# A hybrid streaming encoder step: how the first rows are loaded and summed, a second plain unit in layer 0's output projection, and the last sums and stores

## The chip, the cores and the metric

The kernel runs on one core of a Trainium2 chip. The metric is the device time of one execution, in microseconds, smaller being better. Where the text says PE, DVE, ACT, POOL and SP, it means the five engines as the profile names them: PE multiplies matrices, DVE does elementwise work, ACT applies functions of one input, POOL is a second and slower elementwise engine, and SP issues transfers. Every engine works through its own list of instructions strictly in order.

## The reference

The model is one recurrent layer and one attention layer on 544 tokens (512 of a prompt and 32 of a running stream), 2048 features wide, in float32:

```python
def rms_norm(x, g):                       # over the 2048 features of a token
    return x * lax.rsqrt(jnp.mean(x * x, axis=-1, keepdims=True) + EPS) * g

# layer 0
proj = rms_norm(x, norm_rec) @ w_in_rec            # 2048 -> 2048 + 2048 + 1024 + 1024
xa, ga, xb, gb = split(proj)
ya = rg_lru(causal_conv(xa))                       # gated linear recurrence over time
yb = pool_mix(xb)                                  # trailing means, a map per group
x  = x + concat([ya * silu(ga), yb * silu(gb)]) @ w_out_rec      # 3072 -> 2048
# layer 1
q, k, v, gt = split(rms_norm(x, norm_att) @ w_in_att)            # 2048 -> 4 * 2048
x  = x + (stick_breaking_attention(q, k, v) * silu(gt)) @ w_out_att
y  = rms_norm(x, norm_final)
```

The outputs are `y`, the keys and values, and the last states of the recurrence, the convolution and the pooling.

## The kernel before

Features lie on the 128 partitions and the 544 tokens along the free axis, so that a matrix of 2048 features is 16 "rows" of 128 x 544. A token half has 272 columns. Every float32 operand of a big matmul is split into a rounded high part and a low part (`wsplit`, `split`, `xsplit`: ACT makes the high part, DVE subtracts to get the low one), and one product is three matmuls (`mm3`, L107 to L110: high by high, high by low, low by high).

The projections go by **units** of two blocks of 128 output features by two token halves. A `plain_unit` does, for each of the first 12 input rows, two blocks, two halves and three matmuls, in chunks of 6 rows; a `unit` replaces the 8 block products of these 12 rows by 7, Strassen's way, with sums and differences of weight blocks (DVE, L385 to L400) and of input quarters. Those sums of inputs are made once for each input matrix by `sums_by_pairs`: its loads fetch quarter blocks from DRAM in three rounds, its makes form three sums a round (L283 to L285) and split them (L230, L231), and `three` makes a fourth (L299). The tiles are named T1 to T4 (`xh`, `xl` on the page). Input rows past the 12th are the `xp` rows, done by `rest` plainly. Weight chunks come into a pool of 7 raw buffers (`wraw`), and their split parts into 3 pairs (`wh`, `wl`). Accumulators are 4 PSUM banks (`pp`).

The program is written in a tile framework which inserts the waits and orders each engine's list by a schedule of its own; `tc.high_priority()` draws an instruction forward in it. **Hooks**, a dictionary from a place in a unit to functions, put other work at the chunks of a unit (L329 `run`).

Four stretches matter here.

- **Start.** Unit 0 (`plain_unit(srcs[0], keep, ...)`, L648) needs the 16 rows of x, scaled by `norm_rec`. `load_x` (L489) takes a buffer of an 8-buffer pool (`T`), loads a row, and makes its scaled high and low parts. `squares` (ACT, L483) puts each row's squares into a tile of a 5-buffer pool (`ev`), and `add_squares` sums over the features on PE: `rstd_add` (L137) multiplies by a two-column matrix of ones, 5 token blocks for each of the 16 rows. `rstd_sums` then computes 1/rms (L148 to L153) and diagonal matrices of it (L158), and `rstd_spread` (L168, L170) multiplies these by ones, which puts 1/rms of every token on all partitions; it is copied into `rbc`. Unit 0's results are kept unscaled until then.
- **Layer 0's output projection.** `u == 0` is a plain unit whose hooks bring in the 12 `xp` rows (16 of the 21 `T` buffers hold eight of them for good) and also run the loads and makes of the sums. `u == 1` to 7 are Strassen units.
- **Start of attention.** Head 0 begins with a plain unit; its hooks load and split the `xp` rows, run the sums of x2g (`one`, `two`, `three`), and at places 3 and 4 `rstd_sums` and the copy of the spread 1/rms to `rbc`, which every result of the unit is multiplied by (L449).
- **End.** The last output projection leaves 4 rows, done for 16 blocks in the first token half and then in the second (L1148). Each block's sum is squared on ACT and added to `sqacc` by POOL (L1165), but the last, whose squares stay by themselves; `finish` multiplies by 1/rms and stores on SP's queue (L1142). In the second half, the first half's 16 finishes run beside the matmuls, and the second half's 16 come after them.

## Time and profile before

| what | value |
|---|---|
| median of three runs | 2011.17 us (2004.25, 2011.17, 2015.48) |
| profiled execution, its own time | 2008.65 us |
| its span, first to last instruction | 2006.9 us |
| PE busy | 1941.0 us, 97% |
| DVE busy | 1446.4 us, 72% |
| ACT busy | 919.3 us, 46% |
| POOL busy | 261.6 us, 13% |
| mean granted PE clock | 0.98 |

The span and the execution's own time differ by 1.75 us. A busy PE does not mean that it works at its best pace, since overlapping matmuls and a lowered clock both count as busy; the number of instructions in a stretch, the (x...) of the view by stretches, tells more. PEclk there is the granted share of the full PE clock. In a row of the timeline, the bracket at the end gives the idle time before the instruction and what ended it.

### The profile page before, as it was taken

How to read it: one execution, taken by the hardware profiler on the slowest of the kernel's cores; microseconds unless marked ns; L12 is line 12 of the kernel's file. 1: busy time of each engine (PE TensorE's matmuls, PEld its weight loads, DVE VectorE, ACT ScalarE, POOL GpSimd, SP SyncE). 2: the span in 40 equal slices, each digit the busy share in tenths (PEclk: the TensorE clock that was granted, in tenths of full speed). 3: DMA queues.
4: the chain of work that ended last, by engine and by line, in shares of the span. 5: the costliest groups of instructions: out<-in, count | busy, mean ns of one | idle time of the engine just before them, and what ended most of it. 6: DMA issues, size and time to landing. Idle time of an engine off the chain costs nothing.

```text
span 2006.9 us, 37651 instructions
## 1 busy us (share of the span) xinstructions
PE 1941.0 (97%) x15082; PEld 1919.6 (96%) x15082; DVE 1446.4 (72%) x2318; ACT 919.3 (46%) x1284; POOL 261.6 (13%) x369
## 2 busy tenths in 40 slices
PE   8999999999999889999799999999999999999996
PEld 8999999998999789999799999999999999999996
DVE  4465668669888665556788888888888888874347
ACT  5466666665434443334444453444444444442233
POOL 0021113112010000101111110110111101110013
PEclk8899999999999989999899999999999999999998
DMA  5254434333335654446433343333333333365334
GB/s 181 63 157 144 141 117 137 101 88 103 106 105 179 206 151 141 144 142 212 137 101 102 118 126 103 101 112 116 98 105 107 121 106 101 101 213 183 106 99 148
DMA packets 129951, 257.04 MB, mean 128 GB/s; under 512 B 15920, under 2 KB 40752, under 8 KB 129776
## 3 DMA queue, kind: packets, MB, share of 16 engines
q1 hardware_dynamic: 129696, 254.37, 42.0%
q8 instruction: 118, 1.93, 0.4%
q14 instruction: 57, 0.47, 0.1%
q0 software_dynamic: 80, 0.28, 0.0%
HBM read 217.64 MB, written 36.95 MB: 127 GB/s over the span
## 4 chain that ended last, share of the span: by engine, by line
PE 76%; DVE 12%; issue 5%; DMA 5%; ACT 1%; POOL 0%; SPq 0%; DVEq 0%; ACTq 0%; POOLq 0%
PE pp L108 23%; PE pp L110 23%; PE pp L109 23%; DVE wl L204 3%; DMA wraw<-in_w_in_att 2%; PE pg L137 1%; DMA wraw<-in_w_in_rec 1%; DVE xl L231 1%; DMA T<-x2g 1%; PE pm L109 1%; DVE big L898 1%; PE pm L110 1%; PE pm L108 1%; PE pa L915 1%; DVE e L447 1%
## 5 line engine op out<-in xcount | busy, mean ns | idle before, releaser
L108 PE MATMUL pp<-xh,wh 128*128 128x272 f32 x3180 | 925.4, 292 | 21.0 <-ACT xh L230 10.7
L110 PE MATMUL pp<-xh,wl 128*128 128x272 f32 x3180 | 921.3, 290 | 4.2 <-DVE wl L204 3.9
L109 PE MATMUL pp<-xl,wh 128*128 128x272 f32 x3180 | 921.0, 290 | 1.3 <-DVE xl L231 1.3
L203 ACT ACTIVATE wh<-wraw 128x768 fp32r<-128x768 f32 (+2 forms) x622 | 485.1, 782 | 839.5 <-PE pp L109 603.8
L204 DVE TENSOR_TENSOR wl<-wraw,wh 128x768 fp32r<-128x768 f32 (+2 forms) x622 | 546.2, 881 | 240.1 <-ACT wh L203 237.4
L108 PEld LDWEIGHTS pp<-xh,wh 128*128 128x128 f32 x3180 | 605.2, 191 | 23.7 <-ACT xh L230 11.6
L110 PEld LDWEIGHTS pp<-xh,wl 128*128 128x128 f32 x3180 | 604.2, 190 | 7.0 <-DVE wl L204 6.8
L109 PEld LDWEIGHTS pp<-xl,wh 128*128 128x128 f32 x3180 | 605.0, 190 | 3.2 <-DVE xl L231 2.1
L110 PE MATMUL pp<-xp,wl 128*128 128x272 f32 x1152 | 334.3, 290 | 2.5 <-DVE wl L204 2.2
L108 PE MATMUL pp<-xp,wh 128*128 128x272 f32 x1152 | 332.3, 290 | 3.0 <-ACT xp L230 3.0
L109 PE MATMUL pp<-xp,wh 128*128 128x272 f32 x1152 | 332.1, 289 | 0.0
L108 PEld LDWEIGHTS pp<-xp,wh 128*128 128x128 f32 x1152 | 218.9, 191 | 4.4 <-ACT xp L230 3.3
L110 PEld LDWEIGHTS pp<-xp,wl 128*128 128x128 f32 x1152 | 218.8, 190 | 3.6 <-DVE wl L204 3.6
L109 PEld LDWEIGHTS pp<-xp,wh 128*128 128x128 f32 x1152 | 218.3, 190 | 0.2 <-DVE xp L231 0.2
L447 DVE TENSOR_TENSOR e<-pp,e 128x272 f32<-128x272 f32 x156 | 65.6, 438 | 42.5 <-PE pp L110 37.9
L408 DVE TENSOR_TENSOR e<-pp,e 128x272 f32<-128x272 f32 x184 | 75.4, 430 | 5.6 <-PE pp L110 4.6
L109 PE MATMUL pp<-T,wh 128*128 128x272 f32 x256 | 73.0, 288 | 0.0
L110 PE MATMUL pp<-T,wl 128*128 128x272 f32 x256 | 72.9, 287 | 0.0
L108 PE MATMUL pp<-T,wh 128*128 128x272 f32 x256 | 71.9, 288 | 0.0
L230 ACT ACTIVATE xh<-T 128x544 fp32r<-128x544 f32 x72 | 46.5, 654 | 52.7 <-DVE T L283 18.2
L209 ACT ACTIVATE T<-T 128x544 fp32r<-128x544 f32 (+1 forms) x72 | 45.1, 646 | 44.1 <-DMA T<-in_cv 16.1
L231 DVE TENSOR_TENSOR xl<-T,xh 128x544 fp32r<-128x544 f32 x72 | 51.7, 735 | 12.7 <-ACT xh L230 12.5
(242 smaller groups left out, 2141.3 us busy)
## 6 DMA issues: line engine op xcount, KB each, us to landing
wraw<-in_w_in_att SPq DMA_DIRECT2D x128, 384.0 KB, 3.5
wraw<-in_w_in_rec SPq DMA_DIRECT2D x96, 384.0 KB, 3.4
wraw<-in_w_out_rec SPq DMA_DIRECT2D x64, 384.0 KB, 3.4
wraw<-in_w_in_att SPq DMA_DIRECT2D x64, 256.0 KB, 3.3
wraw<-in_w_in_rec SPq DMA_DIRECT2D x48, 256.0 KB, 3.3
wraw<-in_w_out_att SPq DMA_DIRECT2D x32, 384.0 KB, 4.0
T<-in_xT SPq DMA_DIRECT2D x44, 272.0 KB, 4.6
T<-mixd SPq DMA_DIRECT2D x36, 272.0 KB, 4.5
```

The lines of the kernel that those rows point to most:

```text
L108: nc.tensor.matmul(out, wh, xh, start=start, stop=False)
L109: nc.tensor.matmul(out, wh, xl, start=False, stop=False)
L110: nc.tensor.matmul(out, wl, xh, start=False, stop=stop)
L137: nc.tensor.matmul(ps[:, 1, 256 + 2 * c:258 + 2 * c], a[:, st:st + P], ones[:, :2], start=first and c == 0, stop=last and c == n - 1)
L203: nc.scalar.activation(hi, src, AF.Copy)
L204: nc.vector.tensor_tensor(lo, src, f(hi), ALU.subtract)
L209: nc.scalar.activation(a, src, AF.Copy)
L230: nc.scalar.activation(h, src, AF.Copy)
L231: nc.vector.tensor_tensor(l, src, f(h), ALU.subtract)
L408: nc.vector.tensor_tensor(sm[name], acc[p], sm[other], ALU.add)
L447: nc.vector.tensor_tensor(src, bk, addend, ALU.add)
L898: nc.vector.tensor_tensor_scan(inc[:, o:o + w][:, ::-1], s, s, 1.0, ALU.mult, ALU.min)
```

## The change

Four edits, each in one of the four stretches.

1. **Start.** All 16 rows of x are loaded without an arithmetic instruction between them, into six tiles that lie where the sums T1 to T3 will be later (`room`), and not into the `T` pool; the six weight chunks of unit 0 are issued between them. Scaling (`scale_rows`) comes afterwards and at the hooks. The sum of squares is formed by adding tiles: ACT squares a row, DVE adds it to `sqacc` (`sq_add(..., eng=nc.vector)`), and PE multiplies by ones once, 5 blocks in all, inside `rstd_sums`. `rest` can now take an early chunk.
2. **Output projection of layer 0.** `u == 1` is a plain unit too, and carries the loads and makes of the sums that were in `u == 0`; `three` moves to `u == 2`.
3. **Start of attention.** `rstd_sums` moves from hook 3 of head 0 to hook 1, and `rbc` is copied by ACT with priority instead of by DVE.
4. **End.** The additions to `sqacc` go from POOL to DVE; the squares of the last two blocks (before: of the last one) stay by themselves and are summed by PE; in the second half, odd blocks are stored from ACT's queue and even ones from SP's.

```diff
@@ -334,7 +334,7 @@
-    def rest(src, m, accs, starts, hooks):
+    def rest(src, m, accs, starts, hooks, early=()):
 
         n = len(XP)
         step = n // -(-n // NS)
@@ -342,7 +342,7 @@
             if c:
                 run(hooks, (m, c))
             with tc.high_priority():
-                hi, lo = wsplit(raw(src[:, 2 * NS + c:2 * NS + c + step]))
+                hi, lo = wsplit(early.pop(0) if early else raw(src[:, 2 * NS + c:2 * NS + c + step]))
             for j in range(step):
                 xh, xl = XP[c + j]
                 for acc, hs, st in zip(accs, (H1, H2), starts):
@@ -364,7 +364,7 @@
         for m in range(2):
             run(hooks, 4 + m)
             if more:
-                rest(srcs[m], m, accs[2 * m:2 * m + 2], (False, False), hooks)
+                rest(srcs[m], m, accs[2 * m:2 * m + 2], (False, False), hooks, early)
             for hf in range(2):
                 out(2 * m + hf, accs[2 * m + hf], None)
 
@@ -471,47 +471,51 @@
         xgd = dp.tile([P, 2 * NS, N], F32, tag="xgd", name="xgd")
         for s in (B11, B12, B21, B22):
             fresh(s)
+        rps = two_banks()
         xraw = []
-
-        rps = two_banks()
-        blocks = token_blocks(0, N)
-        sqs = {}
+        room = [xs.tile([P, 3, N], F32, tag=f"{q}{s}", name=nm("xraw")) for s in (T1, T2, T3) for q in ("xh", "xl")]
+
+        def load_rows(k0, k1):
+            for k in range(k0, k1):
+                xraw.append(room[k // 3][:, k % 3, :])
+                nc.sync.dma_start(xraw[k], xT[:, k, :])
+
+        def scale_rows(k0, k1):
+            for k in range(k0, k1):
+                xk, gk = xraw[k], vcol("norm_rec", k)
+                if k < 2 * NS:
+                    j = k % NS
+                    parts = [(XH[s][:, j, :], XL[s][:, j, :], h)
+                             for s, h in zip((B11, B12) if k < NS else (B21, B22), (H1, H2))]
+                else:
+                    hi, lo = fresh_row(k - 2 * NS)
+                    parts = [(hi, lo, slice(0, N))]
+                for hi, lo, h in parts:
+                    nc.scalar.activation(hi, xk[:, h], AF.Identity, scale=gk)
+                    nc.vector.scalar_tensor_tensor(lo, xk[:, h], gk, f(hi), ALU.mult, ALU.subtract)
 
         def squares(k0, k1):
             for k in range(k0, k1):
-                sqs[k] = ev()
-                nc.scalar.activation(sqs[k][:, :N], xraw[k], AF.Square)
-
-        def add_squares(k0, k1):
-            for k in range(k0, k1):
-                rstd_add(rps, blocks, sqs[k], k == 0, k == KT - 1)
-
-        def load_x(k):
-            xk = T()
-            nc.sync.dma_start(xk, xT[:, k, :])
...
-            xraw.append(xk)
-
-        def load_rows(k0, k1):
-            for k in range(k0, k1):
-                load_x(k)
-
-        early = [raw(w_in_rec[0, :, :NS])]
-        load_rows(0, 6)
-        early.append(raw(w_in_rec[1, :, :NS]))
-        squares(0, 5)
-        load_rows(6, 8)
-        early.append(raw(w_in_rec[0, :, NS:2 * NS]))
+                sq_add(k, xraw[k], eng=nc.vector)
+
+        def chunk(m, c):
+            early.append(raw(w_in_rec[m, :, c * NS:min((c + 1) * NS, KT)]))
+
+        early = []
+        load_rows(0, 1)
+        chunk(0, 0)
+        load_rows(1, 6)
+        chunk(1, 0)
+        load_rows(6, 9)
+        chunk(0, 1)
+        load_rows(9, 12)
+        chunk(1, 1)
+        load_rows(12, KT)
+        chunk(0, 2)
+        chunk(1, 2)
+        scale_rows(0, 6)
 
         def scaled_row(k):
 
@@ -646,12 +650,12 @@
 
         srcs = [(w_in_rec[2 * u], w_in_rec[2 * u + 1]) for u in range(24)]
         plain_unit(srcs[0], keep, {
-            1: lambda: (add_squares(0, 5), early.append(raw(w_in_rec[1, :, NS:2 * NS])), load_rows(8, 11), squares(5, 9)),
-            2: lambda: (add_squares(5, 9), load_rows(11, 14), squares(9, 13)),
-            3: lambda: (add_squares(9, 13), load_rows(14, 16), squares(13, 16)),
-            4: lambda: add_squares(13, 16)}, early=early)
+            1: lambda: scale_rows(6, 9), 2: lambda: (scale_rows(9, 12), squares(0, 3)),
+            3: lambda: (scale_rows(12, KT), squares(3, 6)), 4: lambda: squares(6, 9),
+            5: lambda: squares(9, 12)}, early=early)
+        squares(12, KT)
         box = []
-        hk = {0: decay_rates, 1: lambda: box.append(rstd_sums(rps, 0, N, [])),
+        hk = {0: decay_rates, 1: lambda: box.append(rstd_sums(rps, 0, N)),
               2: lambda: (nc.vector.tensor_copy(rbc, rstd_spread(rps, box[0])), late0()),
               4: lambda: back(0, c0)}
         one, two, three = sums(xgd)
@@ -823,14 +827,18 @@
                     1: lambda: (made_rows(), mixed_rows(4, 7)),
                     2: lambda: (made_rows(), mixed_rows(7, 10)),
                     3: lambda: (made_rows(), mixed_rows(10, 12)),
-                    4: lambda: (made_rows(), load(), loads[0]()),
-                    (0, 6): lambda: (makes[0](), loads[1]()),
-                    5: lambda: (makes[1](), loads[2]()),
-                    (1, 6): lambda: (makes[2](), lastload())})
+                    4: lambda: (made_rows(), load())})
+            elif u == 1:
+                plain_unit(srcs, out, {
+                    0: loads[0],
+                    1: lambda: (makes[0](), loads[1]()),
+                    2: lambda: (makes[1](), loads[2]()),
+                    3: lambda: makes[2](),
+                    4: load, 5: lastload})
             else:
                 hk = {2: load}
-                if u == 1:
-                    hk[1] = three
+                if u == 2:
+                    hk[0] = three
                 last = u == KT // 2 - 1
                 if last:
                     quarters(x2g, hk)
@@ -1045,9 +1053,14 @@
             if h == 0:
                 rps = att_tile()
                 box = []
-                with_hooks(ha, {0: [lambda: pend.append(rows(x2g))], 1: [one, lambda: pend.pop()()], 2: [two],
-                                3: [lambda: box.append(rstd_sums(rps, 0, N)), three],
-                                4: [lambda: nc.vector.tensor_copy(rbc, rstd_spread(rps, box[0]))]})
+
+                def spread_rbc():
+                    with tc.high_priority():
+                        nc.scalar.activation(rbc, rstd_spread(rps, box[0]), AF.Copy)
+                with_hooks(ha, {0: [lambda: pend.append(rows(x2g))],
+                                1: [lambda: box.append(rstd_sums(rps, 0, N)), one, lambda: pend.pop()()],
+                                2: [two], 3: [three],
+                                4: [spread_rbc]})
             else:
                 with_hooks(ha, {1: [lambda: (v_turn(prev), w_turn(prev))], 4: [lambda: av(h - 1, prev)]})
             if hh == 0 and G > 0:
@@ -1139,17 +1152,18 @@
             plain_unit(srcs, out, with_hooks({}, hk), more=False)
         pend.pop()()
 
-        def finish(m, hf, r):
+        def finish(m, hf, r, queue=nc.sync):
             s = (H1, H2)[hf]
             o = x3[m][:, s]
             nc.vector.scalar_tensor_tensor(o, o, vcol("norm_final", m), r, ALU.mult, ALU.mult)
-            nc.sync.dma_start(y[:, m, s], o)
+            queue.dma_start(y[:, m, s], o)
 
         for hf, s in enumerate((H1, H2)):
+            accs = [sqacc]
             for m in range(KT):
                 ps = bank()
                 if hf == 1 and m == 2:
-                    rst = rstd_sums(rps, 0, HN, accs)
+                    rst = rstd_sums(rps, 0, HN, done)
                 if hf == 1 and m == 6:
                     nc.scalar.activation(rbc[:, H1], rstd_spread(rps, rst), AF.Copy)
                 with tc.high_priority():
@@ -1159,22 +1173,22 @@
                 nc.vector.tensor_tensor(x3[m][:, s], x3[m][:, s], ps, ALU.add)
                 if m == 0:
                     nc.scalar.activation(sqacc[:, s], x3[m][:, s], AF.Square)
-                elif m < KT - 1:
+                elif m < KT - 2:
                     sq = e()
                     nc.scalar.activation(sq, x3[m][:, s], AF.Square)
-                    nc.gpsimd.tensor_tensor(sqacc[:, s], sqacc[:, s], sq, ALU.add)
+                    nc.vector.tensor_tensor(sqacc[:, s], sqacc[:, s], sq, ALU.add)
                 else:
-                    last = T()
-                    nc.scalar.activation(last[:, s], x3[m][:, s], AF.Square)
-                    accs = [sqacc, last]
+                    accs.append(T())
+                    nc.scalar.activation(accs[-1][:, s], x3[m][:, s], AF.Square)
                 if hf == 1 and m >= 8:
                     finish(2 * (m - 8), 0, rbc[:, H1])
                     finish(2 * (m - 8) + 1, 0, rbc[:, H1])
+            done = accs
             rps = att_tile()
         rst = rstd_sums(rps, HN, N, accs)
         r = rstd_spread(rps, rst)
         for m in range(KT):
-            finish(m, 1, r)
+            finish(m, 1, r, (nc.sync, nc.scalar)[m % 2])
 
 
 # ---- launch ---------------------------------------------------------------
```

**Where the instructions stand.** Outside the four stretches the lists of all engines agree. Three places show the difference.

PE at the start of the program, before: after the first 36 matmuls (unit 0, first chunk), the products of the squares with ones (`pg<-ones,ev`, five each) stand between the matmuls (`pp`).

```order
L110 MATMUL pp_196<-xh_3_111,wl_200 128x272
L137 MATMUL pg_117<-ones,ev_158 128x2 x5
L108 MATMUL pp_197<-xh_1_109,wh_292 128x272
L137 MATMUL pg_117<-ones,ev_160 128x2 x5
L109 MATMUL pp_197<-xl_2_110,wh_292 128x272
L110 MATMUL pp_197<-xh_1_109,wl_293 128x272
L108 MATMUL pp_198<-xh_3_111,wh_292 128x272
```

And now: one such group is left, after 228 matmuls (the 192 of unit 0 and 36 of unit 1), and the spread of 1/rms follows 36 matmuls later.

```order
L110 MATMUL pp_500<-xh_3_111,wl_543 128x272
L137 MATMUL pg_117<-ones,sqacc 128x2 x5
L108 MATMUL pp_501<-xh_1_109,wh_601 128x272
...
L110 MATMUL pp_502<-xh_3_111,wl_602 128x272
L168 MATMUL pg_117<-big_593,ones 128x128 x4
L170 MATMUL pg_117<-big_593,ones 128x32
```

So 75 small products are gone from PE, and 264 big matmuls stand ahead of the spread, as before. What PE waits for at L137 is now the last addition to `sqacc`; DVE's list holds the additions between the splits of the next unit's weights (`wl`):

```order
L123 TENSOR_TENSOR sqacc<-sqacc,ev_448 128x544
L204 TENSOR_TENSOR wl_602<-wraw_599,wh_601 128x768
L123 TENSOR_TENSOR sqacc<-sqacc,ev_451 128x544
L559 TENSOR_SCALAR lt_509<-lt_509 128x16
L123 TENSOR_TENSOR sqacc<-sqacc,ev_454 128x544
```

DVE in layer 0's output projection, before: the second and third round of sums (`T`) stand in one piece, with no weight split between them, in front of unit 1's next weight split.

```order
L231 TENSOR_TENSOR xl_1152_8001<-T_8015,xh_1151_8000 128x544
L283 TENSOR_TENSOR T_8079<-T_8079,T_8075 128x544
L284 TENSOR_TENSOR T_8075<-T_8075,T_8077 128x544
L231 TENSOR_TENSOR xl_1154_8003<-T_8079,xh_1153_8002 128x544
L285 TENSOR_TENSOR T_8077<-T_8079,T_8077 128x544
L231 TENSOR_TENSOR xl_1150_7999<-T_8075,xh_1149_7998 128x544
...
L204 TENSOR_TENSOR wl_8323<-wraw_8320,wh_8322 128x768
```

And now, inside the plain unit 1, each round has splits of that unit's weights around and between its sums:

```order
L204 TENSOR_TENSOR wl_8335<-wraw_8332,wh_8334 128x768
L283 TENSOR_TENSOR T_8134<-T_8134,T_8130 128x544
L284 TENSOR_TENSOR T_8130<-T_8130,T_8132 128x544
L231 TENSOR_TENSOR xl_1162_8120<-T_8134,xh_1161_8119 128x544
L285 TENSOR_TENSOR T_8132<-T_8134,T_8132 128x544
L231 TENSOR_TENSOR xl_1158_8116<-T_8130,xh_1157_8115 128x544
L204 TENSOR_TENSOR wl_8390<-wraw_8387,wh_8389 128x768
```

The sums are now ahead of unit 2, which is the first to use them, and not in the middle of unit 1.

DVE at the start of attention, before: the steps to 1/rms (`rs`) and its diagonals (`big<-ident,rs`) are spread among the sums of x2g.

```order
L148 TENSOR_SCALAR rs_71<-pa_10953 128x5
L204 TENSOR_TENSOR wl_11280<-wraw_11277,wh_11279 128x512
L283 TENSOR_TENSOR T_11012<-T_11012,T_11008 128x544
L284 TENSOR_TENSOR T_11008<-T_11008,T_11010 128x544
L150 RECIPROCAL rs_73<-rs_72 128x5
...
L151 TENSOR_TENSOR rs_74<-rs_73 128x5
L299 TENSOR_TENSOR T_11117<-T_11117,xh_1575_11086 128x544
...
L158 TENSOR_SCALAR big_11176<-ident,rs_73 128x128 x5
```

And now: they stand together, ahead of the `xp` rows and of all sums.

```order
L148 TENSOR_SCALAR rs_71<-pa_10866 128x5
L204 TENSOR_TENSOR wl_11112<-wraw_11109,wh_11111 128x768
L150 RECIPROCAL rs_73<-rs_72 128x5
L151 TENSOR_TENSOR rs_74<-rs_73 128x5
L152 SCALAR_TENSOR_TENSOR rs_74<-rs_74,rs_71 128x5
L153 SCALAR_TENSOR_TENSOR rs_73<-rs_74,rs_73 128x5
L158 TENSOR_SCALAR big_10932<-ident,rs_73 128x128 x5
L231 TENSOR_TENSOR xp_10957<-T_10871,xp_10956 128x544
```

On PE the spread moved with them, from behind the plain unit's last matmul to its second chunk.

11 lines of the change are left out of this document (removed).

## The prediction

> **What bounds the kernel now.** I began with the span in 40 slices, to see where PE is not at its best, then took the view by stretches for those slices, and in each stretch the timeline and the groups, to find what PE waited for.
>
> ```profile
> PE   8999999999999889999799999999999999999996
> PEclk8899999999999989999899999999999999999998
> ```
>
> PE is full in nearly all slices, so it is the bound; what can be won lies in slices 0, 1, 13, 14, 19 and 39. The change's four stretches are just these. The view by stretches (time, busy time and instruction count of each engine, granted PE clock, DMA share, GB/s) prices them:
>
> ```profile
> core 0: us, PE busy (x) PEld busy (x) DVE busy (x) ACT busy (x) POOL busy (x), PEclk, DMA share, GB/s
> 0.00:40.00 40.00, 32.75 (x187) 32.38 (x187) 19.51 (x60) 21.38 (x42) 1.33 (x25) 0.79 0.63 218
> 40.00:80.00 40.00, 40.00 (x281) 40.00 (x281) 12.47 (x27) 14.39 (x24) 1.04 (x3) 0.83 0.17 51
> 680.00:720.00 40.00, 28.08 (x166) 26.23 (x166) 25.92 (x39) 16.36 (x26) 1.87 (x1) 0.83 0.59 176
> 960.00:1000.00 40.00, 26.17 (x185) 25.74 (x184) 33.27 (x59) 18.33 (x28) 2.10 (x3) 0.79 0.42 134
> 1000.00:1040.00 40.00, 40.00 (x322) 39.87 (x321) 32.63 (x51) 16.86 (x22) 4.34 (x6) 1.00 0.32 92
> 1960.00:2006.90 46.90, 30.58 (x233) 29.38 (x231) 36.45 (x80) 17.12 (x36) 13.74 (x15) 0.84 0.45 147
> ```
>
> Undisturbed, PE does 322 matmuls in 40 us: 0.1244 us each. At 40 to 80 it is "busy" throughout but does 281, at clock 0.83: busy there does not mean fast. All times below are of the profiled execution (2008.65 us); it lies 2.5 us under the median of the three runs, which spread over 11 us, and I add nothing for that.
>
> **Start.** The groups up to 75 us, the spread of 1/rms (L168), three stretches of 5 us, and one row of PE's and one of SP's timeline (start, duration, line, operands, count, idle before):
>
> ```profile
> L137 PE MATMUL pg<-ones,ev 128*128 128x2 f32 x160 | 23.2, 270 | 0.0
> L502 DVE SCALAR_TENSOR_TENSOR xl<-T,vec,xh 128x272 fp32r<-128x272 f32 x24 | 10.3, 495 | 4.8 <-ACT xh L501 4.8
> L502 DVE SCALAR_TENSOR_TENSOR xp<-T,vec,xp 128x544 fp32r<-128x544 f32 x4 | 3.0, 780 | 0.4 <-ACT xp L501 0.2
> L204 DVE TENSOR_TENSOR wl<-wraw,wh 128x768 fp32r<-128x768 f32 (+1 forms) x10 | 9.0, 902 | 23.7 <-ACT wh L203 23.7
> L168 PE MATMUL pg<-big,ones x8: 271/275/275, 75.0 to 75.8; 128*128 128x128 f32 x8
> 10.00:15.00 5.00, 5.00 (x33) 5.00 (x33) 4.76 (x16) 5.00 (x11) 0.00 (x0) 1.00 1.04 392
> 25.00:30.00 5.00, 5.00 (x25) 5.00 (x25) 0.33 (x1) 0.99 (x2) 0.00 (x0) 0.53 0.00 0
> 40.00:45.00 5.00, 5.00 (x42) 5.00 (x42) 1.31 (x3) 1.10 (x3) 0.19 (x1) 1.00 0.02 4
> 7.25 1.01 PE L108 MATMUL pp<-xh,wh 128*128 128x272 f32 x2 [7.25 <-ACT xh L501]
> 30.77 3.90 SPq L491 DMA_DIRECT2D T<-in_xT  x8
> ```
>
> The last eight rows of x are not even asked for until 30.77, because a weight load ahead of them in SP's list waits for a buffer; from 25 to 30 nothing moves at all. Meanwhile PE makes two-column products, a whole 128x128 weight load for each, and its clock stands at 0.53. Before the spread at 75.0 stand 264 big matmuls, which at the full pace take 264 x 0.1244 = 32.8 us; with 7.3 us of idleness ahead, the other 75 - 7.3 - 32.8 = 35 us are the small products (23.2 by their row) and half clock: clocks of 0.79 and 0.83 over 40 us each mean (0.21 + 0.17) x 40 x 2 = 30 us at half, in which 15 us are lost (some of these inside the small products' row).
>
> Now: the same 264 matmuls, 7.3 us of idleness (the first row's load and scaling are still what it takes to begin), 2.4 us for some 23 matmuls at half clock until it rises, as I read it from 33 matmuls instead of 40 in 10 to 15, and one group of five doubled small products, 10 of 160 records, 1.2 us. PE alone would reach that group, behind 228 matmuls, at 7.3 + 2.4 + 28.4 = 38.1. But the group needs the last addition on DVE, and these 15 additions are new there:
>
> ```profile
> L284 DVE TENSOR_TENSOR T<-T,T 128x544 f32<-128x544 f32 x3 | 2.2, 719 | 0.0
> ```
>
> A 128x544 sum of two tiles takes 0.72: 10.8 us. In front of the last one DVE also has the low parts (10.3 + 3.0), some nine weight splits (8.1) and small work (about 2): 34 us, from 7.3 on, so 41 if DVE never starves. PE waits about 3 us, does 36 matmuls (4.5 us) while DVE forms the diagonals, and spreads at about 47: **28 us** earlier. With no wait for DVE and some overlap it is 31. The bad end is 18: DVE starves for 5 us (it waited 4.8 and 0.4 for ACT before) and PE's clock falls in that wait. The loads are no limit, as the 16 rows (4.5 MB) and six chunks (2.1 MB) at 392 GB/s take 17 us and now stand in one run, ahead of the rows' use. ACT's 16 squares only move.
>
> [...]
>
> **Output projection.** Unit 1's PE rows, and the two DVE sums that PE waited for, then the unit's end:
>
> ```profile
> 691.65 0.39 PE L108 MATMUL pp<-xh,wh 128*128 128x272 f32 x1 [1.03 <-DVE T L806]
> 698.81 0.82 PE L108 MATMUL pp<-xh,wh 128*128 128x272 f32 x2 [4.63 <-ACT xh L230]
> 704.41 0.39 PE L108 MATMUL pp<-xh,wh 128*128 128x272 f32 x1 [1.58 <-ACT xh L230]
> 713.42 0.59 PE L108 MATMUL pp<-xh,wh 128*128 128x272 f32 x1 [4.14 <-ACT xh L230]
> 702.95 0.72 DVE L283 TENSOR_TENSOR T<-T,T 128x544 f32<-128x544 f32 x1 [3.43 <-DMA T<-mixd]
> 711.96 0.72 DVE L283 TENSOR_TENSOR T<-T,T 128x544 f32<-128x544 f32 x1 [4.05 <-DMA T<-mixd]
> 744.35 0.81 DVE L806 TENSOR_TENSOR T<-T,pp 128x272 f32<-128x272 f32 x2 [2.36 <-PE pp L110]
> ```
>
> Unit 1 stops for each round of sums, whose loads of quarter blocks come late, about 9 us apart. Its 270 matmuls are worth 33.6 us but took 744.3 - 691.7 = 52.6, with spells of half clock after each stop. The change gives up one of eight products (18 more matmuls, 2.2 us) and needs no sum: 288 x 0.1244 = 35.8, a gain of 16.8. The sums remain on DVE, in unit 1, and weight splits of the same unit are queued behind the ones that wait for a load (0.87 to 0.95 us each, 3 pairs of buffers as slack). Three rounds 9 us apart fit into 36 us; I charge 2.3 us for splits made late by a waiting sum: **14.5 us**. Good end 16.8 plus the 1.0 at its head, 18; bad end 8, if two of the three stops (4.6 and 4.1 us) come back through the weight splits.
>
> **Attention.**
>
> ```profile
> 972.04 0.29 PE L110 MATMUL pp<-xp,wl 128*128 128x272 f32 x1
> 984.12 2.05 PE L168 MATMUL pa<-big,ones 128*128 128x128 f32 x8 [11.80 <-issue]
> 988.47 0.56 PE L108 MATMUL pp<-xh,wh 128*128 128x272 f32 x1 [2.04 <-DVE T L449]
> 1000.90 0.29 PE L109 MATMUL pp<-xl,wh 128*128 128x272 f32 x1
> 967.87 0.18 DVE L150 RECIPROCAL rs<-rs 128x5 f32<-128x5 f32 x1
> 978.44 0.16 DVE L151 TENSOR_TENSOR rs<-rs 128x5 f32<-128x5 f32 x1
> 983.75 1.06 DVE L158 TENSOR_SCALAR big<-ident,rs 128x128 f32<-128x128 f32 x5
> ```
>
> PE ends the plain unit at 972.3 and has nothing until 1/rms is spread at 984.1; all four banks wait to be multiplied by it. The chain on DVE starts in time, but its short steps (0.15 to 0.18) stand in line behind sums: 10.6 us between two of them. Together, and ahead of the sums, the chain should be over before the unit is. PE's stop of 11.8 + 2.0 goes, and with it the slow restart (0.79 over this stretch). It does not all become gain: DVE, 33.3 of 40 us busy here, has the same sums to make before PE can go on into the Strassen part, and the chain was not what delayed these. Counting its list as it now stands from about 966.5 on (18 sums and splits at no more than the 0.72 of the row above, 4 weight splits at 0.90, 5 results of 272 columns at about 0.42), the sums of the second quarter are ready at about 985. The products that use these end at 1000.90 before, some 100 matmuls behind the stop; they would end at about 990. From these 11 us I take 3 off for the backlog that DVE carries into the next part: **8 us**. Ends: 4 (DVE is the bound through the whole stretch, only the second stop and the slow clock go), 13 (the whole stop goes). The copy to `rbc`, 0.71 on DVE, costs ACT, 18 of 40 us busy, nothing.
>
> **Tail.**
>
> ```profile
> 1974.99 0.49 DVE L1145 SCALAR_TENSOR_TENSOR T<-T,vec,rbc 128x272 f32<-128x272 f32 x1
> 1976.59 1.01 DVE L1145 SCALAR_TENSOR_TENSOR T<-T,vec,rbc 128x272 f32<-128x272 f32 x1
> 1990.36 0.83 PE L137 MATMUL pa<-ones,sqacc 128*128 128x2 f32 x6 [2.51 <-POOL sqacc L1165]
> 1995.41 4.17 DVE L1145 SCALAR_TENSOR_TENSOR T<-T,vec,pa 128x272 f32<-128x272 f32 x10 [1.17 <-PE pa L170]
> 1995.93 4.75 SPq L1146 DMA_DIRECT2D out_y<-T  x10
> 2000.78 3.12 SPq L1146 DMA_DIRECT2D out_y<-big  x6
> ```
>
> PE's last sum waits 2.5 us for POOL; that goes. DVE takes over 28 additions of 272 columns, about 0.42 each (10 finishes of that size take 4.17): 14 in this half, 5.9 us, on an engine busy 36.45 of 46.9; against that, finishes that coincide with POOL take twice as long (1.01 against 0.49), and this goes. SP issues 16 stores in 7.9 us; DVE's 16 finishes at 0.42 take 6.7, so two queues save at most 1.2. Sum of +2.5, +1.2 and about +2 of collisions, less DVE's part that isn't hidden (about 4): **1.5 us**; between 4 (all additions hidden) and -1.
>
> [...]
>
> **Sum.** 28 + 14.5 + 8 + 1.5 = 52; 2008.65 - 52 = **1957 us**. All good ends: 66, 1943. All bad ends: 18 + 8 + 4 - 1 = 29, 1980.
>
> **Rivals.**
>
> - *Half clock stays in the start.* If the slow spells belong to something other than the small products and the stops (the first microseconds of any program, say), 15 us are still lost, the spread comes at 62 instead of 47, and the sum is 37: 1972. For it: the clock is below 1 in 30 of the first 80 us. Against: in 40 to 45 it is 1.00 again, so it is no matter of age. Chance 0.12.
> - *DVE becomes the bound in three places.* The additions make 34 us of DVE work in a row at the start (gain 20), sums block splits in unit 1 (8), backlog in attention (4), nothing in the tail: 32, so 1977. For it: DVE is 83% busy in 960 to 1000. Against: in 40 to 80 it is 31% busy. Chance 0.18.
> - *Slower: PE's clock falls.* With its pauses gone, PE works without rest; if the granted clock over the rest (1941 us busy) fell by 52/1941 = 2.7%, from 0.98 to 0.955, all is lost, and beyond 3.3% it is slower than 2020. Against it: 1000 to 1040 has PE full and clock 1.00. Chance 0.02.
> - *The change doesn't do what it says.* Rows of x could still wait on SP. In the new list of SP they stand behind one another with only fresh buffers between, so this is in the 0.12 of the first rival's time.
>
> **How the numbers follow.** Forecast 0.63, its own range 1948 to 1968; all terms at their good ends 0.05 (1943); the rivals 0.12, 0.18 and 0.02. The range 1944 to 1977 leaves out the slow case, half of the fast one, and the upper part of the DVE case. A difference under 0.5% (10 us) can't be told from no change here, so faster means under 2001 and slower over 2021. Every case but the third rival is well under 2001: faster 0.96, same 0.025, slower 0.015.
>
> **What would show it.** Start: L168 at 44 to 50 us instead of 75, L137 with 10 rows in place of 160, and a clock near 1.00 in 15 to 80; a wait of PE at L137 for DVE's `sqacc` over 5 us shows the second rival. Output projection: no stop over 2 us within unit 1, some 320 matmuls in 680 to 720 (shifted). Attention: no idle time ahead of L168; PE's idle before the Strassen part under 4 us. Tail: L1145 at 0.4 to 0.5 throughout, L137 released by ACT or DVE in under 1 us. What would make it wrong: a spread later than 57, PE idle in unit 1 behind DVE's `wl` (L204), or a mean clock below 0.98.

## The result, and the profile after

The changed kernel takes 1954.53 us (median of four runs, 1951.20 to 1959.63), the kernel before 2009.39 in the runs beside it (four runs, 2004.25 to 2015.48): a ratio of 0.9728, 95% interval 0.9692 to 0.9764, 54.9 us less where 52 were forecast. The profiled executions differ by 2008.65 - 1951.20 = 57.4 us, and so do the spans (2006.9 and 1949.5).

The profile's page of the changed kernel, busy tenths of PE and granted clock in 40 slices:

```profile
PE   8999999999999999999999999999999999999997
PEclk9999999999999999999999999999999999999998
```

The dips in slices 1, 13, 14 and 19 are gone; what is left is the first slice and the last. The view by stretches of the changed kernel (busy time and count of each engine, PE clock, DMA share, GB/s):

```profile
core 0: us, PE busy (x) PEld busy (x) DVE busy (x) ACT busy (x) POOL busy (x), PEclk, DMA share, GB/s
0.00:40.00 40.00, 32.94 (x242) 32.67 (x243) 33.39 (x78) 32.05 (x61) 1.51 (x26) 1.00 0.72 248
40.00:80.00 40.00, 40.00 (x323) 40.00 (x321) 28.02 (x55) 26.70 (x36) 8.17 (x10) 1.00 0.37 99
660.00:700.00 40.00, 38.57 (x308) 38.57 (x309) 30.57 (x44) 17.15 (x26) 2.73 (x2) 1.00 0.64 199
920.00:960.00 40.00, 37.22 (x286) 35.85 (x285) 37.39 (x61) 22.14 (x32) 11.37 (x6) 1.00 0.44 133
```

And the kernel before, over the 40 us that stand for 660 to 700 there:

```profile
690.00:730.00 40.00, 27.23 (x159) 25.36 (x159) 30.20 (x48) 16.49 (x25) 1.87 (x1) 0.83 0.56 167
```

PE does 308 matmuls in place of 159 in the output projection's unit 1, and 323 in place of 281 at 40 to 80, at a clock of 1.00 in both. DVE is now busy 33.4 of the first 40 us (19.5 before): it took the additions over.

Where the time came from is read by looking up the same PE instruction in both timelines and taking the difference of its start:

| the same instruction of PE | before, us | after, us | difference |
|---|---|---|---|
| first big matmul | 7.25 | 7.06 | 0.2 |
| a gate product of the recurrence, behind unit 1 and others | 333.68 | 302.73 | 31.0 |
| first of the output projection's unit 1 | 691.65 | 661.43 | 30.2 |
| first of its unit 2 | 744.51 | 697.56 | 47.0 |
| shortly before attention | 950.03 | 904.25 | 45.8 |
| in head 0, behind its Strassen part | 1076.85 | 1021.34 | 55.5 |
| 60 us before the end | 1939.91 | 1883.72 | 56.2 |
| end of the last big matmul | 1987.84 | 1931.00 | 56.8 |
| span | 2006.9 | 1949.5 | 57.4 |

So the start gives 31, the output projection 15.6 (unit 2 gives 1.2 of the 16.7 back), attention some 10, the end about 1.

The start in the changed kernel: the groups of small products and of additions, the spread of 1/rms, the last addition on DVE and PE's one group of small products:

```profile
L137 PE MATMUL pg<-ones,sqacc 128*128 128x2 f32 x10 | 1.2, 243 | 0.0
L123 DVE TENSOR_TENSOR sqacc<-sqacc,ev 128x544 f32<-128x544 f32 x15 | 10.9, 724 | 0.1
L168 PE MATMUL pg<-big,ones x8: 271/275/275, 44.0 to 44.8; 128*128 128x128 f32 x8
37.51 0.73 DVE L123 TENSOR_TENSOR sqacc<-sqacc,ev 128x544 f32<-128x544 f32 x1
38.41 1.17 PE L137 MATMUL pg<-ones,sqacc 128*128 128x2 f32 x10
```

The last addition ends at 38.24 and PE arrives at 38.41: no wait at all, but no slack on DVE either. At the start of attention, the chain on DVE, the copy on ACT, and three of the four waits of about 1 us that PE has left there (the fourth, 0.95, is ahead of the sum over the features, for POOL):

```profile
909.47 0.18 DVE L150 RECIPROCAL rs<-rs 128x5 f32<-128x5 f32 x1
909.69 0.20 DVE L151 TENSOR_TENSOR rs<-rs 128x5 f32<-128x5 f32 x1
914.54 0.61 ACT L1059 ACTIVATE rbc<-pa 128x544 f32<-128x544 f32 x1
929.82 0.36 PE L108 MATMUL pp<-xh,wh 128*128 128x272 f32 x1 [0.94 <-DVE T L449]
937.25 0.39 PE L108 MATMUL pp<-xh,wh 128*128 128x272 f32 x1 [1.43 <-ACT xh L230]
969.81 0.39 PE L110 MATMUL pp<-xh,wl 128*128 128x272 f32 x1 [0.96 <-DVE wl L204]
```

The two steps that stood 10.6 us apart are 0.22 apart, 1/rms is spread while the plain unit runs, and the stops of 11.8 and 2.0 us have become 0.9 and 1.4.

### The profile page after: what moved, and what is told of

It is laid out like the page before. It is cut to its first block, busy times and chain, and to the rows that moved or that the text cites. A ratio compares the mean times of both kernels' runs of the same rounds, so it can differ in the third digit from the quotient of the medians.

```text
span 1949.5 us, 37355 instructions
## 1 busy us (share of the span) xinstructions
PE 1907.7 (98%) x14962; PEld 1886.7 (97%) x14962; DVE 1449.8 (74%) x2343; ACT 915.5 (47%) x1281; POOL 242.7 (12%) x341
## 4 chain that ended last, share of the span: by engine, by line
PE 49%; DVE 9%; DMA 4%; issue 3%; ACT 1%; POOL 0%; SPq 0%; DVEq 0%; ACTq 0%; POOLq 0%
PE pp L108 15%; PE pp L110 15%; PE pp L109 15%; DVE wl L204 3%; DMA wraw<-in_w_in_att 2%; DVE big L906 1%; PE pm L109 1%; DMA T<-x2g 1%; DVE xl L231 1%; PE pm L110 1%; PE pm L108 1%; PE pa L923 1%; DMA T<-mixd 1%; ACT wh L203 0%; PE pa L109 0%
## 5 line engine op out<-in xcount | busy, mean ns | idle before, releaser
L209 ACT ACTIVATE T<-T 128x544 fp32r<-128x544 f32 (+1 forms) x72 | 45.2, 645 | 46.1 <-DMA T<-in_cv 17.5
L1091 POOL COPY kn<-T 128x32 f32<-128x32 f32 x16 | 20.6, 1286 | 326.9 <-DVE T L449 326.9
```

The lines of the kernel that those rows point to most:

```text
L209: nc.scalar.activation(a, src, AF.Copy)
L1091: nc.gpsimd.tensor_copy(kn[:, hh, :], k_[:, SEQ:])
```

## The experiments

Each kernel is a change to the changed kernel, and a difference is against it unless another is named. A single execution moves by some 2 us for no reason of the edit: with only the end changed back, the shift went from -0.6 us at 1000 to 1.5 at 1900, where all lists agree. Small shifts are therefore read from the stretch itself.

### Each edit undone

**The first edit undone**: the lines of the start as they were.

```diff
-        load_rows(0, 1)
-        chunk(0, 0)
...
+        early = [raw(w_in_rec[0, :, :NS])]
+        load_rows(0, 6)
...
```

> The changed kernel with its first edit undone: rows of x loaded through the 8-buffer pool as before, squares summed on PE by 80 two-column products. Theory (the start's gain is its own and nothing later takes it back): the spread of 1/rms is at 75 us again, against 44.0 in the changed kernel, every later landmark is 31 us later, and the time is 1954.5 + 31 = 1985. Rival (later waits, above all on DVE, had part of this time as slack): the shift shrinks behind the first units and the time is under 1975.

Measured: 1981.29 us (ratio to before 0.9844, 0.9821 to 0.9867), 26.8 more. In the traces the spread is late by 30.7 (74.7 to 75.5 against 44.0 to 44.8):

```profile
L168 PE MATMUL pg<-big,ones x8: 270/275/275, 74.7 to 75.5; 128*128 128x128 f32 x8
```

and the shift is 30.6 at 100 us and 30.5 at 1900 us: nothing later takes it back.

**The second edit undone**: unit 1 is a Strassen unit, and the loads and makes of the sums are in unit 0 again.

```diff
-            elif u == 1:
-                plain_unit(srcs, out, {
-                    0: loads[0],
...
-                if u == 2:
-                    hk[0] = three
+                if u == 1:
+                    hk[1] = three
```

> The changed kernel with the output projection's edit undone: unit 1 is a Strassen unit again and the sums are loaded and made in unit 0. Theory (unit 1 waited for the rounds of sums; a plain unit needs none): stops of 4 to 5 us in front of two chunks of unit 1 come back, unit 1 takes 52 us instead of 36, and the time is 1954.5 + 15.5 = 1970. Rival (what counted was which time stood ahead of it: with the start 31 us shorter the stops change): under 1962.

Measured: 1974.87 us (0.9814, 0.9788 to 0.9840), 20.3 more. PE's stops in unit 1 are back, about as long as they were:

```profile
668.72 0.82 PE L108 MATMUL pp<-xh,wh 128*128 128x272 f32 x2 [4.64 <-ACT xh L230]
674.52 0.59 PE L108 MATMUL pp<-xh,wh 128*128 128x272 f32 x1 [1.29 <-ACT xh L230]
683.64 0.59 PE L108 MATMUL pp<-xh,wh 128*128 128x272 f32 x1 [4.61 <-ACT xh L230]
```

Unit 1 takes 661.56 to 714.74, 53.2 us against 36.1. So an earlier start does not change these stops: loads and makes belong to unit 0 and are carried along with it. The shift is 16.4 before attention, 18.2 at 1000 us and 23.4 at the end. The last 5 us are lost within attention, where the order of every engine's instructions is the same as in the changed kernel. From 1000 us on PE waits 4.2 us for DVE's weight splits, against 1.7 in the changed kernel; why, stays open.

**The third edit undone**:

```diff
...
-                                1: [lambda: box.append(rstd_sums(rps, 0, N)), one, lambda: pend.pop()()],
-                                2: [two], 3: [three],
-                                4: [spread_rbc]})
+                with_hooks(ha, {0: [lambda: pend.append(rows(x2g))], 1: [one, lambda: pend.pop()()], 2: [two],
+                                3: [lambda: box.append(rstd_sums(rps, 0, N)), three],
+                                4: [lambda: nc.vector.tensor_copy(rbc, rstd_spread(rps, box[0]))]})
```

> The changed kernel with the edit at the start of attention undone. Theory: PE stands still for about 12 us ahead of the spread of 1/rms and for 2 us behind it, and the time is 1954.5 + 10.3 = 1965 (10.3 is the difference of the two traces over this stretch). Rival (DVE is the bound of this stretch and only the first stop's half clock went): 1958 to 1960.

Measured: 1964.06 us (0.9765, 0.9744 to 0.9787), 9.5 more; the stretch itself 12.0 more. The stop is back:

```profile
939.79 2.04 PE L168 MATMUL pa<-big,ones 128*128 128x128 f32 x8 [13.28 <-issue]
```

**The last edit undone**: additions on POOL, one tile of squares by itself, stores from SP alone.

> The changed kernel with the last edit undone (additions on POOL, one tile of squares by itself, all stores from SP). Theory: from the last big matmul to the span's end 1 to 2 us more than the changed kernel's 18.5, PE's first sum waits for POOL again, and the time is 1956, which three rounds can't tell from 1954.5. Rival (the additions on DVE cost more than they save, and the two queues bring the gain): no difference or 1 us less behind the last matmul, and the finishes in the last 20 us at 0.9 to 1.0 us each again.

Measured: 1956.25 us (0.9724, 0.9701 to 0.9747), 1.7 more, which is within what can be told. The four differences, 26.8 + 20.3 + 9.5 + 1.7, add up to 58.3, where the whole is 54.9. The kernel before took 2014.01 in the runs beside these four, 4.6 more than beside the changed kernel; by the ratios to it the four are worth about 23, 17, 7 and -1 us, 47 in all. So it is not shown more closely than some 8 us either way whether the edits take from one another.

### What made the start slow

**Rows up front, squares on PE.** The loads of the changed kernel, the sums of the kernel before:

```diff
-                sq_add(k, xraw[k], eng=nc.vector)
+                sq = ev()[:, :N]
+                nc.scalar.activation(sq, xraw[k], AF.Square)
+                rstd_add(rps, blocks, sq, k == 0, k == KT - 1)
...
```

> The changed kernel, but the squares are summed on PE again (80 two-column products, 160 records), while the rows of x are still loaded up front. Theory (the small products cost their time and lower the granted clock, whether or not loads are late): the spread of 1/rms comes at 66 us or later, against 44.0, and the clock is under 0.9 in part of 15 to 65. Rival (late loads starved PE, and the clock fell for that): PE does the 160 records at the full clock, 18.7 us, the spread is at 44 + 18.7 - 1 = 62 at most, and the clock stays 1.00.

**The same with 128 columns of ones** in each small product:

```diff
...
-                rstd_add(rps, blocks, sq, k == 0, k == KT - 1)
+                flat = rps.rearrange("p a b -> p (a b)")
+                for c, st in enumerate(blocks):
+                    nc.tensor.matmul(flat[:, c * P:(c + 1) * P], sq[:, st:st + P], ones,
+                                     start=k == 0 and c in (0, 4), stop=k == KT - 1 and c in (3, 4))
```

> As the run with squares summed on PE, but each small product has 128 columns of ones instead of 2 (same number of products and records, the same sums, 64 times over). Theory (two columns leave the array idle behind each weight load, and the clock is granted by the array's work): the clock is 1.00 behind the first microseconds, and the spread is not later than with two columns, at 60 to 66, though each product does 64 times the arithmetic. Rival (any product whose weights are used once lowers the clock, or the clock has another cause): clock and time as with two columns, or worse.

First the run with two columns, then that with 128: the group of small products, the spread, and 5 us of the view by stretches.

```profile
L137 PE MATMUL pg<-ones,ev 128*128 128x2 f32 x160 | 23.2, 276 | 0.0
L168 PE MATMUL pg<-big,ones x8: 271/275/275, 72.1 to 72.9; 128*128 128x128 f32 x8
35.00:40.00 5.00, 5.00 (x25) 5.00 (x25) 0.96 (x1) 2.60 (x4) 0.00 (x0) 0.50 0.26 68
```

```profile
L510 PE MATMUL pg<-ones,ev 128*128 128x128 f32 x160 | 19.0, 275 | 0.0
L171 PE MATMUL pg<-big,ones x8: 271/275/275, 60.3 to 61.1; 128*128 128x128 f32 x8
35.00:40.00 5.00, 5.00 (x45) 5.00 (x44) 0.96 (x1) 2.06 (x4) 0.00 (x0) 1.00 0.26 80
```

With the rows loaded early the spread comes at 72.1 instead of 75.0: by themselves the loads were worth 3 us, though the kernel before asked for eight rows only at 30.77. With 128 columns, 64 times the arithmetic, it comes at 60.3, at a clock of 1.00 in every 5 us up to 80; times of one execution each were 1979.68 and 1967.56. So 31 us are 2.9 for the loads, 11.8 for the clock, and 16.3 for the small products' own time, in the order in which these runs take them away. These are single executions, and each share can be off by about 1 us: the slow first matmuls of the program last until 12.6 us in the kernel before, 13.6 with two columns and 11.7 with 128, though the edit between these two comes later in PE's list. The additions on DVE without the early loads were not tried; with the last rows asked for at 30.77 they would have had little time.

### Which half of the third edit matters

**The copy on DVE, without priority**, the chain in hook 1:

```diff
-                    with tc.high_priority():
-                        nc.scalar.activation(rbc, rstd_spread(rps, box[0]), AF.Copy)
+                    nc.vector.tensor_copy(rbc, rstd_spread(rps, box[0]))
```

> The changed kernel, but rbc is copied by DVE without priority at the start of attention; the chain to 1/rms stays in hook 1. Without the priority the spread stands 82 PE instructions later, 48 ahead of where it was before the change. Theory (what counted is that the chain's short steps stood among the sums on DVE): PE's stop ahead of the spread stays away, and the stretch is 0 to 4 us longer than in the changed kernel. Rival (the copy with priority on ACT carries the gain): 8 us or more.

**The chain in hook 3**, the copy on ACT with priority:

```diff
-                with_hooks(ha, {0: [lambda: pend.append(rows(x2g))],
-                                1: [lambda: box.append(rstd_sums(rps, 0, N)), one, lambda: pend.pop()()],
-                                2: [two], 3: [three],
+                with_hooks(ha, {0: [lambda: pend.append(rows(x2g))], 1: [one, lambda: pend.pop()()], 2: [two],
+                                3: [lambda: box.append(rstd_sums(rps, 0, N)), three],
```

> The changed kernel, but the chain to 1/rms starts at hook 3 of head 0 as before; the copy stays on ACT with priority. Theory: the chain stands among the sums again, PE stops for 10 us or more ahead of the spread, and the stretch is about 10 us longer than in the changed kernel. Rival (priority draws the chain forward anyway): under 4 us longer.

Rows of the run with the copy on DVE:

```profile
927.33 1.05 PE L168 MATMUL pa<-big,ones 128*128 128x128 f32 x8
943.94 0.56 PE L108 MATMUL pp<-xh,wh 128*128 128x272 f32 x1 [9.36 <-DVE T L449]
942.10 0.71 DVE L1058 COPY rbc<-pa 128x544 f32<-128x544 f32 x1
943.37 1.47 DVE L449 TENSOR_TENSOR T<-pp,rbc 128x272 f32<-128x272 f32 x4
```

My expectation was wrong here. PE no longer waits ahead of the spread, but the stop is only moved: the spread is there at 928.5, and the copy stands 13.6 us behind it, in DVE's list behind the sums, with the four results behind it. The stretch is 9.3 us longer, the time 1962.60. With the chain in hook 3 the stop ahead of the spread is back:

```profile
945.88 2.05 PE L168 MATMUL pa<-big,ones 128*128 128x128 f32 x8 [13.55 <-issue]
```

and the stretch is 13.3 us longer (1969.95). Of the 12.0 us that the whole edit is worth in this stretch, the chain alone keeps 2.7 and the copy alone none (each in one execution): here the chain was as late as its last link. Whether the early copy needs ACT, or only the priority, was not tried apart.

### What the last edit consists of

**The additions on POOL again**, all else of the edit kept:

```diff
-                    nc.vector.tensor_tensor(sqacc[:, s], sqacc[:, s], sq, ALU.add)
+                    nc.gpsimd.tensor_tensor(sqacc[:, s], sqacc[:, s], sq, ALU.add)
```

> The changed kernel with the additions to sqacc back on POOL in the end; two tiles of squares by themselves and two store queues stay. From the last big matmul's end to the span's end the kernel before has 19.05 us, the changed one 18.5, the one with the whole edit undone 19.04; and from that matmul to DVE's last finish 15.2 in the changed kernel against 14.5 with the edit undone. Theory (the additions cost on DVE what the queues save): DVE is done about 14.5 us after the last matmul, the span's end is 17.5 to 18, so the additions were better left on POOL. Rival (the collisions with POOL cost as much as the additions): 18.5 or more.

**All stores from SP**:

```diff
-            finish(m, 1, r, (nc.sync, nc.scalar)[m % 2])
+            finish(m, 1, r)
```

> The changed kernel with all stores of the end on SP's queue; the additions stay on DVE. Theory: DVE's last finish comes 15.2 us after the last big matmul as in the changed kernel, but the span's end 4.6 us behind it instead of 3.3, so 19.8 in all: the second queue is worth 1.3 us and is the whole gain of this edit. Rival (issue was never the limit): 18.5.

DVE's last finishes with the additions on POOL (span 1953.4, last big matmul over at 1935.90), and then with all stores on SP (span 1952.6, 1932.76), with SP's last stores:

```profile
1947.66 2.53 DVE L1158 SCALAR_TENSOR_TENSOR big<-big,vec,pa 128x272 f32<-128x272 f32 x6
```

```profile
1945.45 2.54 DVE L1158 SCALAR_TENSOR_TENSOR big<-big,vec,pa 128x272 f32<-128x272 f32 x6
1946.74 2.86 SPq L1159 DMA_DIRECT2D out_y<-big  x6
```

From the last big matmul to DVE's last finish, and from there to the span's end:

| kernel | additions | store queues | to the last finish | from there | sum |
|---|---|---|---|---|---|
| before | POOL | 1 | 14.2 | 4.9 | 19.1 |
| last edit undone | POOL | 1 | 14.5 | 4.6 | 19.0 |
| additions on POOL | POOL | 2 | 14.3 | 3.2 | 17.5 |
| all stores from SP | DVE | 1 | 15.2 | 4.6 | 19.8 |
| changed | DVE | 2 | 15.2 | 3.3 | 18.5 |
| changed, a second time | DVE | 2 | 15.9 | 3.3 | 19.1 |

The second queue is worth 1.3 us in both pairs that differ in it alone (4.59 to 3.25 and 4.61 to 3.27), and the additions cost 0.8 to 1.6 on DVE: the edit's two halves nearly cancel behind the last matmul. The seven other runs of this study that have the changed kernel's end take 18.5 to 18.9, so the combination with additions on POOL and two queues has the shortest end, by 1 to 1.6 us; its whole time in one execution, 1955.14, can't show that (with all stores on SP 1954.29).

An addition to `sqacc` takes 0.88 us on POOL in the kernel before (28 of them) and 0.43 on DVE in the changed one (26). The collisions with POOL show, but they fall while PE still has matmuls to do: ahead of the last one, DVE's finishes take 0.74 us on the average where POOL adds and 0.50 where DVE does; behind it they take about 0.5 in either.

### A version with three things more

Twelve products of ones with ones ahead of everything, meant to have PE at its full pace when the first big matmul starts; 1/rms of layer 0 a chunk later; six finishes moved behind the last block's sum.

```diff
+        for i in range(12):
+            nc.tensor.matmul(rps[:, 0, :P], ones, ones, start=True, stop=True)
...
-        hk = {0: decay_rates, 1: lambda: box.append(rstd_sums(rps, 0, N)),
-              2: lambda: (nc.vector.tensor_copy(rbc, rstd_spread(rps, box[0])), late0()),
+        hk = {0: decay_rates, 2: lambda: box.append(rstd_sums(rps, 0, N)),
+              3: lambda: (nc.vector.tensor_copy(rbc, rstd_spread(rps, box[0])), late0()),
...
-                if hf == 1 and m >= 8:
+                if hf == 1 and 8 <= m < 13:
...
+        for m in range(10, 14):
+            finish(m, 0, rbc[:, H1])
         rst = rstd_sums(rps, HN, N, accs)
+        for m in range(14, 16):
+            finish(m, 0, rbc[:, H1])
```

> The changed kernel with three things more: 12 products of ones with ones on PE ahead of everything (their result is not used), 1/rms of layer 0 one chunk later in unit 1 (hooks 2 and 3 instead of 1 and 2), and the last six finishes of the first token half behind the last block's sum, in the gaps of the chain to 1/rms. Theory: PE's clock is up when the first big matmul starts, which saves 2.4 us, since PE now has 36 more matmuls before it needs DVE's last addition; with the last block's sum no longer behind six finishes the end takes 15.5 us instead of 18.5 behind the last big matmul: 5 us together, about 1949.5. Rivals: DVE, full from 10 to 35 us, is the bound of the start, PE waits there and gains nothing (1952); the finishes in the gaps push the chain's short steps back (1954).

> The changed kernel itself, on the chip on which the version with three things more runs, to compare the two. Theory: 1954, 4 to 5 us above that version. Rival: within 1 us of it.

Measured: 1955.54 (0.9729, 0.9711 to 0.9747) against 1952.89 (0.9713, 0.9696 to 0.9729) for the changed kernel on the same chip. It gains nothing; the intervals overlap. Its first PE rows and stretches:

```profile
1.12 5.04 PE L476 MATMUL pg<-ones 128*128 128x128 f32 x24 [1.12 <-DVE lt L556]
7.31 0.39 PE L108 MATMUL pp<-xh,wh 128*128 128x272 f32 x1 [1.15 <-ACT wh L203]
9.38 0.43 PE L109 MATMUL pp<-xl,wh 128*128 128x272 f32 x1
5.00:10.00 5.00, 3.66 (x19) 3.04 (x19) 3.24 (x9) 3.58 (x8) 0.00 (x0) 0.90 1.01 346
10.00:15.00 5.00, 5.00 (x34) 5.00 (x33) 5.00 (x12) 5.00 (x12) 0.00 (x0) 0.76 1.05 392
```

PE was faster when the first big matmul started (0.39 for the first, 0.60 in the changed kernel), but the 12 products were done at 6.2, PE waited 1.15 us and then had few matmuls at hand, and from about 9.0 to 12.4 us the clock stood at half (the 0.90 and 0.76 of the two stretches): matmuls 0.23 apart, as in the first microseconds of the changed kernel, where the view gives 1.00. At 30 us the two versions stand 0.15 us apart. DVE was not the bound here: its last addition is over at 38.92, and PE wants it at 42.76. The end, 18.4 us behind the last matmul, is next to the changed kernel's own 18.5 to 19.1: PE's first sum waits 2.04 us for DVE's additions as before, and 1/rms is spread 7.0 us behind the last matmul instead of 7.1. No kernel of this study is shown to beat the changed one.

## Why the prediction was right, point by point

- **Start, 28 forecast, 31.0 measured.** The forecast's point that a PE called busy spent these 35 us on small products and half clock holds, and the run with 128 columns (1.00 at 35 to 40 us, where two columns have 0.50) shows that the two-column products were the cause of the half clock. The mis-sized term is DVE's: I let it begin at 7.3 with 34 us of work and end at 41, so that PE would wait 3 us. It was busy from about 6 on, full from 10 to 35, with 31.1 us of work, and ended at 38.24, just ahead of PE (forecast to arrive at 38.1, measured 38.41). That is my good end, 31. That this group may have to wait for DVE was right all the same: among the nine runs with this start as it is, PE's full pace begins anywhere from 10.9 to 13.5 us, yet the small products begin at 38.3 to 38.8 in all of them. In the two runs whose full pace began first, at 10.9 and 11.5, PE waits for the last addition. The first of them, the run with the third edit undone:

```profile
38.30 1.05 PE L137 MATMUL pg<-ones,sqacc 128*128 128x2 f32 x8 [0.55 <-DVE sqacc L123]
```

- **Output projection, 14.5 forecast, 15.6 measured.** Unit 1 takes 36.1 us (35.8 undisturbed by the forecast) and has no stop over 0.2 us behind its first matmul. The 2.3 us that I charged for delayed weight splits were not spent there; 0.6 us more than before were lost at its head and 1.2 in unit 2.
- **Attention, 8 forecast, about 10 measured.** The stops went as forecast. The charge of 3 us for DVE's backlog was right, and the 11 us ahead of it were too few. By the count of PE's big matmuls, the changed kernel is 58.5 us ahead at the products behind its stop for `xh` (996.61 before, 938.10 now); it came with 45.8, so some 12.7 are won. At 1039.12 (983.56 now) it is 55.6 ahead, so 3 are given back, in part to waits for DVE's splits such as the one at 969.81. One sentence was wrong in its weight: that the copy on ACT costs nothing is true, but the prediction left it at that, while the run with the copy on DVE loses 9.3 of the 12.0 us.
- **Tail, 1.5 forecast, about 1.2 measured.** 0.6 before the last matmul's end, 0.6 behind it, though the second time the changed kernel ran the second 0.6 were gone; so the size may be luck. The size of the second queue (1.2 forecast, 1.3 measured), the collisions with POOL and the sign of the additions on DVE are right. DVE took over 26 additions, not the 28 of the forecast, since the squares of one more block in each half stay by themselves. That PE's sum would follow at once is wrong: it waits 2.16 us for DVE where it waited 2.5 for POOL.

```profile
1933.16 0.80 PE L137 MATMUL pa<-ones,sqacc 128*128 128x2 f32 x6 [2.16 <-DVE sqacc L1179]
```

- **The rivals.** Half clock that stays in the start: excluded by the clock of 1.00 there. DVE as the bound in three places: PE waits for it 1.7 us at most in these (ahead of unit 1), but in the start the margin was 0.2 us, and in two other runs there was none. A lower clock over the rest: the mean clock rose from 0.98 to 0.99. The fall of the clock in a wait for DVE, from the start's bad end, did not come either: PE did not wait at the first sum, and the clock is 1.00 in every 5 us from 35 to 50.

## What to carry to other kernels

Where a view calls an engine busy, count its instructions per microsecond: here 160 records with two columns of data, a weight load with each, took 23.2 us of PE's time, and the clock among them stood at 0.50, where 128 columns left it at 1.00. A sum of many tiles is added up on an elementwise engine with idle time and reduced across partitions once (here 15 additions of 0.72 us on DVE, and 10 records on PE in place of 160); the price is that this engine's list is now what the next step waits for, 0.55 us in the run with the third edit undone. A short dependent chain must be drawn out of a long list link by link, the last copy too: here the chain without its copy kept 2.7 of 12 us, and the copy without its chain none.

## What the runs showed of the hardware that I had not expected

The granted clock followed what the products were, not how many. 160 records of 128x2 took 23.2 us, and in the stretches around them the clock went to 0.50; 160 records of 128x128 took 19.0 us at 1.00. Late loads, which I took for a part of the start's slowness, cost 3 us alone.

A pace once reached was soon lost: in the version with three things more, 24 records of ones ahead of everything, 1.15 us of waiting and about 1.6 us of sparse matmuls were followed by 3.4 us at half clock (0.90 in 5 to 10 us and 0.76 in 10 to 15), though PE worked then.

When PE first reaches its full pace was not settled by the program alone: with the same first matmuls, at 7.1 to 7.4 us, it began between 10.9 and 13.5 us. Until then the matmuls stand 0.23 apart or more, and yet the view gives a clock of 1.00 for 5 to 10 and 10 to 15 us, before and after the change. So the forecast's 2.4 us at half clock were read from the pace; the granted clock does not show them.
